# Later table loads, fewer early fill products and a DMA queue in program order in a two-block fp32 transformer kernel

## The chip, the cores and the metric

The kernel runs on one core of one Trainium2 chip. The metric is the device time of one execution in microseconds (us), lower is better. PE is TensorE, DVE VectorE, ACT ScalarE, POOL GpSimd, and SP is SyncE, whose queue issues all the kernel's transfers from HBM.

## The reference

Two blocks follow each other on one sequence of 256 tokens of 1024 features, all in fp32. The first has two layers of window attention and differential attention side by side, between an input product of 1024 x 4096 and an output product. The second has two layers (`DEPTH` is 2): sparse attention in the first, latent attention in the second, each with a cross-attention to a memory of 256 rows, and a block of 16 experts behind each.

```python
for l in range(DEPTH):                               # first block
    h = rmsnorm(x, norm_g[l])
    proj = h @ w_in[l]                               # 1024 x 4096
    ...
    x = x + y @ w_out[l]
x = rmsnorm(x, final_g)
for i in range(DEPTH):                               # second block
    proj = x @ nsa_w_in[j] if kind == 0 else x @ mla_w_in[j]
    ...
    mkv = mem @ mem_w_kv[i]
    xa = memory_cross_attention(xq, mk, mv).reshape(B, S, XA_WIDTH)
    y = jnp.concatenate([mix, xa], -1) @ w_out[i]
    x = layer_norm(DEEPNORM_ALPHA * x + y, ln_g[i, 0], ln_b[i, 0])
    f = hier_moe(x, ...)                             # 16 experts, 2 of them for each token
    x = layer_norm(DEEPNORM_ALPHA * x + f, ln_g[i, 1], ln_b[i, 1])
```

An expert is `silu(x @ w_gate) * (x @ w_up)`, times its gate, `@ w_down`: three matrices of 2 MB, so 96 MB for the 16 experts of a layer.

## The kernel before

**Products.** A projection (`Proj`, line 253 issues its products) splits both sides into a high and a low part that PE multiplies at its fast fp32 rate, and makes three products for each. `Emit.split` makes the weights' parts: ACT casts the high part (`wsp`, line 134), DVE subtracts for the low one (line 135). The parts of the activations are `xTh` (ACT, line 350) and `xTl` (DVE, line 352), made from `xraw`, the transposed input. A step of a `Proj` is one tile of 128 input features; `add_two` runs the first two projections together, four steps of one, four of the other, and so again.

**Order of work.** `Flow` holds a list of steps. `flow.before(s, fn)` calls a function ahead of step `s`, `flow.after` behind it; a step number below zero is a place ahead of the first product. PE, DVE and ACT run in the order in which the code calls them (`manual_schedule(engines=ENGINES)`). SP is not in that set: the framework's scheduler orders its queue. SP issues one transfer after another, and a transfer waits, with all behind it in the queue, until its tile is free and until the eighth transfer ahead of it has landed.

**Tables.** `constants2` loads positions and norm gains (`loads`, at step -10), and computes from the positions the angles of the rotations on DVE, one piece ahead of each of the steps 5 to 11.

**Experts.** The 192 loads of 512 KB of a layer's expert weights are handed out by the class `Weights`. There are three kinds of places: a ring of 12 tiles (`w`), and slots of 512 KB (`b4`) and of 1 MB (`b8`), shared with the activations (both show as `wa`). When a slot's weights have been read, `Weights.read` frees it and loads the next ones into it, as far as `others`, a table of what else will want the slots at which step, allows. When a ring tile has been read, the next load of the ring is called there. How many ring loads are under way is set ahead of the experts: `nsa_layer` calls twelve for the first layer, `mla_layer` three for the second. The tiles are handed out round the ring, so that with three under way the other nine are free.

**Between the layers.** Near the end of the first experts (step 237) `tail[0]` starts `memory_kv`, which loads the memory and its weights and makes `mkv` in small items of two products; `some(n)` in `mla_layer` takes n items at a time to fill PE. `tail[1]` loads the first part of the latent attention's input weights (`w_in`), in the last quarter of the last expert. At the block's end stands a branch (`tc.If`, line 2584) for experts with more than 64 tokens; here it isn't taken, and SP waits at it for the transfers under way.

## Time and profile before

| | us |
|---|---|
| median of 3 runs | 1007.44 (1005.86 to 1008.91) |
| the profiled execution | 1008.35 |
| its span in the trace | 1006.6 |
| PE busy | 978.5 |
| DVE busy | 644.2 |
| ACT busy | 433.4 |
| moved by DMA | 286.66 MB, 285 GB/s over the span |

The time of an execution has 1.75 us more than the span of its trace. PE's busy time and its gaps make up the span; what DVE, ACT and the DMA do counts where PE waits for it. The experts' products begin at 453 us in the first layer and at 783 in the second; the second layer's attention lies from 666 to there, and PE's last product ends at 995.7.

### The profile page before, as it was taken

To read this page: it belongs to the slowest core of one execution; us is meant where nothing else is said; L and a number is where in the kernel's file an instruction comes from. 1 tells how busy PE (TensorE), PEld (TensorE's weight loads), DVE (VectorE), ACT (ScalarE), POOL (GpSimd) and SP (SyncE) were. 2 spreads that over 40 slices of the span, in tenths; PEclk is the share of its full clock that TensorE was granted. 3 is DMA by queue.
4 is the path that set the end of the run, shared out by engine and by line. 5 is a ranking of instruction groups with operands and counts; after the bars stand their busy time and mean duration, and the time that the engine had idled before them with its cause. 6 is when DMAs were issued, how large, how long until landed. Compare 5 with 4: busy or idle time off the path is not lost. (4 is left out here: it accounts for less than half of the span.)

```text
span 1006.6 us, 16077 instructions
## 1 busy us (share of the span) xinstructions
PE 978.5 (97%) x5627; PEld 645.7 (64%) x5627; DVE 644.2 (64%) x1816; ACT 433.4 (43%) x1072; POOL 19.1 (2%) x38
## 2 busy tenths in 40 slices
PE   8999999999999989999999999999999999999994
PEld 7997889888898866784343443368878443434332
DVE  5766886567966788748465545458885656553545
ACT  6556665556664467634212121234883321212121
POOL 0000000000100000000000000000000000000000
PEclk9999999999999999999999999999999999999998
DMA  8964575543576584797999999986698799999995
GB/s 287 377 200 128 155 252 172 164 127 125 157 225 206 154 214 128 225 377 262 379 409 409 408 409 409 399 295 218 210 349 324 273 343 409 408 409 409 408 407 170
DMA packets 110873, 286.66 MB, mean 285 GB/s; under 512 B 14208, under 2 KB 30912, under 8 KB 110272
## 3 DMA queue, kind: packets, MB, share of 16 engines
q1 hardware_dynamic: 110784, 285.55, 79.3%
q8 instruction: 47, 0.77, 0.3%
q14 instruction: 42, 0.34, 0.1%
HBM read 284.46 MB, written 1.05 MB: 284 GB/s over the span
## 5 line engine op out<-in xcount | busy, mean ns | idle before, releaser
L2201 PE MATMUL eg<-wa,xg 128*64 128x512 f32 x796 | 210.6, 597 | 0.2 <-DMA wa<-moe_w_up_dram 0.2
L135 DVE TENSOR_TENSOR wsp<-w,wsp 128x512 fp32r<-128x512 f32 (+4 forms) x256 | 164.8, 658 | 64.0 <-ACT wsp L134 62.6
L253 PE MATMUL pj<-xTh,wsp 128*128 128x256 f32 x768 | 155.2, 292 | 3.5 <-DVE wsp L135 3.2
L134 ACT CAST wsp<-w 128x512 fp32r<-128x512 f32 (+4 forms) x256 | 142.7, 595 | 16.7 <-PE pj L253 7.6
L253 PEld LDWEIGHTS pj<-xTh,wsp 128*128 128x128 f32 x768 | 124.6, 193 | 10.3 <-issue 4.4
L2201 PEld LDWEIGHTS eg<-wa,xg 128*64 128x64 f32 x796 | 60.8, 136 | 102.2 <-issue 90.0
L253 PE MATMUL pj<-xTl,wsp 128*128 128x256 f32 x384 | 109.2, 284 | 0.0
L253 PE MATMUL pj<-wsp,xTh 128*128 128x512 f32 (+3 forms) x352 | 108.4, 389 | 0.0
L2211 DVE SCALAR_TENSOR_TENSOR z<-z,eg 64x512 f32<-64x512 f32 x32 | 21.7, 679 | 133.3 <-ACT z L2208 133.3
L2208 ACT ACTIVATE z<-eg 64x512 f32<-64x512 f32 x32 | 18.9, 592 | 174.5 <-PE eg L2201 174.5
L2241 PE MATMUL dn<-wa,hT 128*64 128x512 f32 x360 | 86.2, 593 | 0.2 <-DMA wa<-moe_w_down_dram 0.2
L2221 DVE SCALAR_TENSOR_TENSOR hq<-z,gall,eg 32x128 f32<-32x128 f32 x240 | 83.3, 347 | 4.1
L253 PE MATMUL pj<-wsp,yTh 128*128 128x512 f32 x240 | 77.7, 405 | 0.0
L2201 PE MATMUL eg<-w,xg 128*64 128x512 f32 x228 | 77.6, 597 | 0.0
L253 PEld LDWEIGHTS pj<-xTl,wsp 128*128 128x128 f32 x384 | 74.2, 193 | 0.4
L2251 ACT CAST ys<-dn 64x512 fp32r<-64x512 f32 x60 | 34.9, 581 | 85.3 <-PE dn L2241 79.8
L253 PEld LDWEIGHTS pj<-wsp,xTh 128*128 128x128 f32 x352 | 62.8, 188 | 11.6 <-issue 2.5
L253 PE MATMUL pj<-wsp,xTl 128*128 128x512 f32 (+3 forms) x176 | 66.7, 379 | 0.0
L2241 PEld LDWEIGHTS dn<-wa,hT 128*64 128x64 f32 x360 | 25.6, 137 | 52.1 <-issue 44.5
L405 ACT ACTIVATE z<-z,mx 128x256 f32<-128x256 f32 (+1 forms) x104 | 48.4, 470 | 15.9 <-DVE mx L396 15.9
L2256 DVE TENSOR_TENSOR ys<-dn,ys 64x512 fp32r<-64x512 f32 x60 | 41.3, 688 | 15.0 <-ACT ys L2251 13.9
L253 PEld LDWEIGHTS pj<-wsp,yTh 128*128 128x128 f32 x240 | 43.1, 188 | 9.1 <-issue 1.6
(424 smaller groups left out, 1440.5 us busy)
## 6 DMA issues: line engine op xcount, KB each, us to landing
wa<-moe_w_up_dram SPq DMA_DIRECT2D x101, 512.0 KB, 10.2
wa<-moe_w_gate_dram SPq DMA_DIRECT2D x98, 512.0 KB, 10.2
wa<-moe_w_down_dram SPq DMA_DIRECT2D x94, 512.0 KB, 10.2
w<-w_in_dram SPq DMA_DIRECT2D x64, 512.0 KB, 4.6
w<-moe_w_down_dram SPq DMA_DIRECT2D x34, 512.0 KB, 10.2
w<-moe_w_gate_dram SPq DMA_DIRECT2D x30, 512.0 KB, 10.2
w<-moe_w_up_dram SPq DMA_DIRECT2D x27, 512.0 KB, 10.1
w<-w_out_dram SPq DMA_DIRECT2D x24, 512.0 KB, 3.7
```

The costliest lines, as they stand in the source:

```text
L134: self.nc.scalar.copy(hi, src)
L135: self.nc.vector.tensor_sub(lo, src, hi)
L253: nc.tensor.matmul(o, a, b, start=begin and i == 0, stop=last and i == 2, skip_group_check=True)
L405: E.nc.scalar.activation(z[i], (src or z)[i], AF.Exp, bias=mx[:, i:i + 1], scale=1.0 if src else -1.0, accum_out=sm[:, i:i + 1])
L2201: self.E.nc.tensor.matmul(self.ps[b * CAP:b * CAP + CAP], self.xg[:, k, self.j], w, start=k == 0, stop=k == KD - 1, skip_group_check=True)
L2208: self.E.nc.scalar.activation(self.th, self.ps[:CAP], AF.Tanh, scale=0.5)
L2211: self.E.nc.vector.scalar_tensor_tensor(self.th, self.th, 1.0, self.ps[:CAP], op0=OP.add, op1=OP.mult)
L2221: self.E.nc.vector.scalar_tensor_tensor(self.hq[32 * q:32 * q + 32, :, h], th[:, q], self.gate()[r], u[:, q], op0=OP.mult, op1=OP.mult)
L2241: self.E.nc.tensor.matmul(self.pd[n * CAP:n * CAP + CAP], self.hT[:, k], self.w[2][k](0)[:, 512 * n:512 * n + 512], start=k == 0, stop=k == 3,
L2251: self.E.nc.scalar.copy(self.y[r, n], self.pd[r])
L2256: self.E.nc.vector.tensor_sub(self.y[o, n], self.pd[r], self.y[r, n])
```

## The change

Four edits. At the start: 8 warm-up products instead of 12, the first weights in two transfers of one feature tile each (`load_first`), `xraw` of the last four feature tiles ahead of the loads of `x`, its parts two and one steps earlier, squares and norm rows a little later, and the tables behind the second half of both first projections, with their angles five steps later. In the second layer's attention: two `mkv` items instead of three in seven opening steps, more in the last steps of the projection `pq`. At the end of the first experts: `tail[1]` is called with `tail[0]`, ahead of the branch, and nine `b4` slots are kept for it instead of five. And SP joins the engines that run in program order in the main part of both blocks of experts.

```diff
@@ -523,15 +523,15 @@
     norm.raw = raw = E.b8((KD, S), "xraw")
     load_xT(0, 2)
     nc.sync.dma_start(ng, a["norm_gT"])
-    E.warm(12)
+    E.warm(8)
     norm.begin()
-    norm.parts(0)
-
-    for s, fn, v in ((-15.7, load_xT, (2, 4)), (-15.5, load_x, (0,)), (-13, load_xT, (4, 8)), (-12.5, load_x, (1,))):
+
+    for s, fn, v in ((-15.8, load_xT, (2, 4)), (-13, load_xT, (4, 8)), (-12.5, load_x, (0,)), (-12.2, load_x, (1,))):
         flow.before(s, fn, *v)
+    flow.before(-3, norm.parts, 0)
     for i in range(4):
-        flow.before((3, 4, 6, 7)[i], norm.squares, i // 2, i % 2)
-    for k, s in ((2, 0), (4, 4), (6, 5)):
+        flow.before(5 + i, norm.squares, i // 2, i % 2)
+    for k, s in ((2, 0), (4, 2), (6, 4)):
         flow.before(s, norm.parts, k)
     fgT = const.tile([P, KD], F32, name="fgT")
     subg = const.tile([P, 2], F32, name="subg")
@@ -638,7 +638,15 @@
           for i, out, feature in ((0, qa_out, True), (1, k_out("ka"), True), (2, v_out("va"), False),
                                   (4, q_out("qb"), True), (5, k_out("kb"), True), (6, v_out("vb"), False),
                                   (3, ga_out, True), (7, gb_out, False))]
-    norm.rows(flow, s0 + 5 if l else s0 + 8, 5 if l else 4)
+    norm.rows(flow, s0 + 5 if l else s0 + 9, 5 if l else 3)
+    if l == 0:
+        def load_first(v, k0, nk):
+            for k in range(0, nk, 1 if k0 == 0 else nk):
+                n = 1 if k0 == 0 else nk
+                w = a["w_in"][0][(k0 + k) * P:(k0 + k + n) * P, :512]
+                nc.sync.dma_start(v[:, k:k + n], w.rearrange("(k p) c -> p k c", p=P))
+
+        ps[0].src = load_first
     Proj.add_two(flow, *ps[:2])
     for p in ps[2:]:
         p.add(flow)
@@ -836,12 +844,12 @@
     t = {}
 
     def loads():
-        nc.sync.dma_start(E.lnT, a["ln_T"])
-        nc.sync.dma_start(E.lnP, a["ln_P"])
         pos_i = const.tile([P, 3], I32, name="pos_i")
         nc.sync.dma_start(pos_i, a["pos"])
         t["pos"] = const.tile([P, 3], F32, name="pos"), pos_i
         t["inv"] = E.bcast(a["inv"], 24, "inv")
+        nc.sync.dma_start(E.lnT, a["ln_T"])
+        nc.sync.dma_start(E.lnP, a["ln_P"])
         t["rows"] = E.b4((S,), "rows")
         for h in range(2):
             nc.sync.dma_start(t["rows"][32 * h:32 * h + 32], a["ln_rows"])
@@ -911,9 +919,9 @@
     nc.scalar.activation(E.sin[:, 0, :16], E.mhalf, AF.Sin)
 
     it = angles()
-    for s in range(5, 12):
+    for s in range(10, 17):
         flow.before(s, next, it, None)
-    for s, fn in ((-10, loads), (13, sines), (15, rows)):
+    for s, fn in ((-7, loads), (17, sines), (19, rows)):
         flow.before(s, fn)
 
 
@@ -1639,7 +1647,7 @@
             E.free(ps)
 
     for _ in range(7):
-        step(lambda: some(3))
+        step(lambda: some(2))
     flow.before(0, rows)
     for i in (1, 0):
         flow.before(2, normalise, i)
@@ -1722,7 +1730,7 @@
     pq = Proj(E, [(0, win[:, 416:672])], 256, lambda: t["xT"], xq_out, True)
     flow.before(0, pq.load)
     for k in range(KD):
-        flow.steps.append((lambda k=k: pq.split(k), lambda k=k: (pq.mm(k), some(int(k < 10)))))
+        flow.steps.append((lambda k=k: pq.split(k), lambda k=k: (pq.mm(k), some(1 + (k > 3)))))
     pq.finish(flow, 23)
     flow.before(17, shared, 0)
     flow.before(18, shared, 1)
@@ -2116,7 +2124,7 @@
         self.others["b4"] += [(228, 2), (229, 1), (238, -2), (245, 1), (257, 2)]
         if i == 0:
             self.others["b8"].append((16 * NE - 19, 1))
-            self.others["b4"].append((16 * NE - 19, 5))
+            self.others["b4"].append((16 * NE - 19, 9))
         for v in self.others.values():
             v.sort(key=lambda e: (e[0], -e[1]))
 
@@ -2439,7 +2447,7 @@
 
             at(pre, s + 40, start)
 
-    with tc.manual_schedule(engines=ENGINES):
+    with tc.manual_schedule(engines=ENGINES | {mybir.EngineType.SP}):
         lg = columns()
         W.fill()
         E.warm(10)
@@ -2536,6 +2544,7 @@
                 work = tail[0]()
                 for g in work:
                     next(g)
+                tail[1]()
         assert not pre and not post, (pre, post)
 
 
@@ -2572,8 +2581,6 @@
             if q == 1:
                 parts(2, Y)
                 E.free(Y.y, *others)
-            if q == 1 and tail:
-                tail[1]()
             if q in (1, 2):
                 for t in range(2):
                     stats(q - 1, t)
```

**The start, ACT's queue.** Rows of before, then of the change, from the first parts of the input on (`wsp` are high parts of weights; `z` squares of `x`).

```order
L350 ACTIVATE xTh<-xraw,ng 128x256 x2
L134 CAST wsp<-w 128x512 x3
L350 ACTIVATE xTh<-xraw,ng 128x256 x2
L134 CAST wsp<-w 128x512 x3
L340 ACTIVATE z,ssq<-x 128x512
L134 CAST wsp<-w 128x512
L340 ACTIVATE z,ssq<-x 128x512
L350 ACTIVATE xTh<-xraw,ng 128x256 x2
L134 CAST wsp<-w 128x512
L350 ACTIVATE xTh<-xraw,ng 128x256 x2
```

```order
L350 ACTIVATE xTh<-xraw,ng 128x256 x2
L134 CAST wsp<-w 128x512 x3
L350 ACTIVATE xTh<-xraw,ng 128x256 x2
L134 CAST wsp<-w 128x512 x2
L350 ACTIVATE xTh<-xraw,ng 128x256 x2
L134 CAST wsp<-w 128x512 x2
L350 ACTIVATE xTh<-xraw,ng 128x256 x2
L134 CAST wsp<-w 128x512
L340 ACTIVATE z,ssq<-x 128x512
L134 CAST wsp<-w 128x512
```

The third pair of `xTh` moved from behind the seventh `wsp` to behind the fifth, and the squares from between the sixth and seventh to behind the eighth.

**The start, DVE's queue.** Rows of before, then of the change, from the fourth `wsp` on.

```order
L135 TENSOR_TENSOR wsp<-w,wsp 128x512 x4
L352 SCALAR_TENSOR_TENSOR xTl<-xraw,ng,xTh 128x256 x2
L135 TENSOR_TENSOR wsp<-w,wsp 128x512
L879 CAST pos<-pos_i 128x3
L881 TENSOR_SCALAR ang<-inv,pos 128x24 x3
L352 SCALAR_TENSOR_TENSOR xTl<-xraw,ng,xTh 128x256 x2
L135 TENSOR_TENSOR wsp<-w,wsp 128x512
```

```order
L135 TENSOR_TENSOR wsp<-w,wsp 128x512 x2
L352 SCALAR_TENSOR_TENSOR xTl<-xraw,ng,xTh 128x256 x2
L135 TENSOR_TENSOR wsp<-w,wsp 128x512 x2
L352 SCALAR_TENSOR_TENSOR xTl<-xraw,ng,xTh 128x256 x2
L135 TENSOR_TENSOR wsp<-w,wsp 128x512 x5
L368 TENSOR_TENSOR ssq<-ssq 128x2
L147 TENSOR_SCALAR rs_r<-ssq 128x2
L374 TENSOR_SCALAR rdiag<-ident,rs_r 128x128 x2
L135 TENSOR_TENSOR wsp<-w,wsp 128x512
L887 CAST pos<-pos_i 128x3
L889 TENSOR_SCALAR ang<-inv,pos 128x24 x3
L135 TENSOR_TENSOR wsp<-w,wsp 128x512
```

The cast of `pos` moved from behind the eighth `wsp` to behind the thirteenth.

**The second layer's attention, ACT's queue.** Rows of before, then of the change, at the last weights of the projection `pq` (`w` of 256) and the first of the next one (288).

```order
L1665 ACTIVATE z,mssq<-cs 128x128
L134 CAST wsp<-w 128x256 x3
L134 CAST wsp<-w 128x288
L1013 COPY mkv<-mkv 128x512
L134 CAST wsp<-w 128x288 x2
L1689 ACTIVATE cTh<-tp,cg 128x256 x3
L134 CAST wsp<-w 128x288
```

```order
L1673 ACTIVATE z,mssq<-cs 128x128
L134 CAST wsp<-w 128x256 x2
L1014 COPY mkv<-mkv 128x512
L134 CAST wsp<-w 128x256
L134 CAST wsp<-w 128x288 x3
L1697 ACTIVATE cTh<-tp,cg 128x256 x3
L134 CAST wsp<-w 128x288
```

The copy of `mkv` here is that of the second half in before and that of the first half now; the second half's moved behind these rows, past the scores on `xq`.

**The last experts, SP's queue.** Rows of before, then of the change, from the 13th load of the layer on (`w` goes to the ring, `wa` to slots).

```order
L2161 DMA wa<-moe_w_gate_dram 128x1024
L2161 DMA wa<-moe_w_up_dram 128x1024
L2161 DMA wa<-moe_w_gate_dram 128x1024
L2161 DMA wa<-moe_w_up_dram 128x1024
L119 DMA w<-moe_w_down_dram 128x1024 x2
L119 DMA wa<-moe_w_down_dram 128x1024 x2
L2161 DMA wa<-moe_w_up_dram 128x1024
L2161 DMA wa<-moe_w_gate_dram 128x1024
L2161 DMA w<-moe_w_gate_dram 128x1024
L2161 DMA wa<-moe_w_gate_dram 128x1024
L2161 DMA w<-moe_w_up_dram 128x1024
L2161 DMA w<-moe_w_gate_dram 128x1024 x2
```

```order
L2169 DMA wa<-moe_w_gate_dram 128x1024
L2169 DMA wa<-moe_w_up_dram 128x1024
L2169 DMA wa<-moe_w_gate_dram 128x1024
L2169 DMA wa<-moe_w_up_dram 128x1024
L119 DMA wa<-moe_w_down_dram 128x1024 x2
L2169 DMA wa<-moe_w_up_dram 128x1024
L2169 DMA wa<-moe_w_gate_dram 128x1024 x2
L2169 DMA wa<-moe_w_up_dram 128x1024
L119 DMA wa<-moe_w_down_dram 128x1024 x2
L2169 DMA wa<-moe_w_up_dram 128x1024
L119 DMA wa<-moe_w_down_dram 128x1024 x2
L2169 DMA wa<-moe_w_gate_dram 128x1024
```

The rows to `w` left this stretch; the `wa` rows stand as before. In the change the fourth load to the ring of this layer comes behind the 46th to slots; in before there are twelve ring loads ahead of that place.

## Rows read from the trace of the kernel before

**Rows 1.** The page: PE's busy time; GB/s in 40 slices of 25.2 us.
```profile
PE 978.5 (97%) x5627; PEld 645.7 (64%) x5627; DVE 644.2 (64%) x1816; ACT 433.4 (43%) x1072; POOL 19.1 (2%) x38
...
GB/s 287 377 200 128 155 252 172 164 127 125 157 225 206 154 214 128 225 377 262 379 409 409 408 409 409 399 295 218 210 349 324 273 343 409 408 409 409 408 407 170
```

**Rows 2.** PE's waits over the span: us in total, times, longest.
```profile
PE pj L253 <- DVE wsp L135: 3.2, 2, 3.0
```

**Rows 3.** Windows: length, busy us of PE, PEld, DVE, ACT, POOL, clock, DMA, GB/s.
```profile
666.00:700.00 34.00, 34.00 (x196) 30.27 (x195) 24.17 (x66) 15.00 (x40) 1.81 (x2) 1.00 0.75 264
700.00:740.00 40.00, 36.05 (x258) 29.89 (x257) 35.16 (x134) 33.16 (x107) 0.92 (x3) 1.00 0.74 238
...
826.00:840.00 14.00, 14.00 (x68) 4.60 (x64) 6.12 (x14) 2.35 (x4) 0.00 (x0) 1.00 1.02 409
...
960.00:980.00 20.00, 19.19 (x80) 7.12 (x75) 8.85 (x18) 4.00 (x7) 0.00 (x0) 1.00 1.03 409
```

**Rows 4.** Timeline of PE, start: start, us, engine, line, operation, [idle before, releaser].
```profile
6.58 0.39 PE L253 MATMUL pj<-xTh,wsp 128*128 128x256 f32 x1 [0.25 <-ACT wsp L134]
...
7.30 0.50 PE L253 MATMUL pj<-xTh,wsp 128*128 128x256 f32 x2 [0.22 <-DVE wsp L135]
...
22.24 0.60 PE L253 MATMUL pj<-xTh,wsp 128*128 128x256 f32 x2 [3.00 <-DVE wsp L135]
```

**Rows 5.** Windows of the start, columns as in rows 3.
```profile
1.50:5.00 3.50, 3.46 (x16) 3.46 (x17) 0.01 (x1) 1.38 (x4) 0.88 (x6) 1.00 0.76 210
5.00:6.00 1.00, 1.00 (x9) 1.00 (x9) 0.88 (x2) 0.45 (x2) 0.00 (x0) 1.00 0.97 340
...
23.50:25.00 1.50, 1.50 (x9) 1.50 (x9) 1.47 (x6) 0.08 (x1) 0.39 (x1) 0.50 1.06 396
```

**Rows 6.** Timeline of DVE, start.
```profile
16.08 0.69 DVE L135 TENSOR_TENSOR wsp<-w,wsp 128x512 fp32r<-128x512 f32 x1
20.00 0.17 DVE L879 CAST pos<-pos_i 128x3 f32<-128x3 int32 x1 [3.23 <-DMA pos_i<-pos_dram]
...
21.50 0.69 DVE L135 TENSOR_TENSOR wsp<-w,wsp 128x512 fp32r<-128x512 f32 x1
```

**Rows 7.** Timeline of ACT, start; a cast behind a wait starts as its weights land.
```profile
11.82 1.15 ACT L134 CAST wsp<-w 128x512 fp32r<-128x512 f32 x2 [1.40 <-DMA w<-w_in_dram]
...
14.64 0.90 ACT L350 ACTIVATE xTh<-xraw,ng 128x256 fp32r<-128x256 f32 x2
...
17.26 0.62 ACT L134 CAST wsp<-w 128x512 fp32r<-128x512 f32 x1 [0.40 <-DMA w<-w_in_dram]
```

**Rows 8.** Timelines of PE, ACT and DVE, the second layer's attention.
```profile
698.17 0.60 PE L998 MATMUL mkv<-wkv,memT 128*128 128x256 f32 x2
...
702.01 1.14 PE L497 MATMUL sc<-mkv,xq 64*128 64x256 f32 x8 [1.88 <-DVE xq L1697]
...
698.80 0.59 ACT L1013 COPY mkv<-mkv 128x512 f32<-128x512 f32 x1 [5.14 <-PE mkv L998]
...
701.27 0.69 DVE L1697 TENSOR_SCALAR xq<-pj 128x512 f32<-128x512 f32 x1
```

**Rows 9.** Timeline of SP's queue, loads of the last experts' weights.
```profile
716.07 0.33 SPq L2161 DMA_DIRECT2D w<-moe_w_up_dram  x1
...
735.49 4.29 SPq L119 DMA_DIRECT2D w<-moe_w_down_dram  x2
...
813.24 0.33 SPq L2161 DMA_DIRECT2D w<-moe_w_up_dram  x1
...
829.69 0.33 SPq L2161 DMA_DIRECT2D wa<-moe_w_gate_dram  x1
830.99 0.33 SPq L2161 DMA_DIRECT2D wa<-moe_w_up_dram  x1
```

**Rows 10.** Timeline of PE, the last experts.
```profile
791.33 7.09 PE L2201 MATMUL eg<-wa,xg 128*64 128x512 f32 x32
...
984.74 1.08 PE L2241 MATMUL dn<-wa,hT 128*64 128x512 f32 x4 [0.23 <-DMA wa<-moe_w_down_dram]
```

## The prediction

> **What bounds the kernel now.** I read the page first: TensorE (PE) is busy for 978.5 us [rows 1] of the span of 1006.6, so a change can win only by closing PE's gaps, 28.1 us in all, and can lose by opening new ones. PE's list of waits says where the largest is: 3.2 us for `pj` on VectorE's `wsp` [rows 2], at the start of the program. Third I read the DMA rate by slices: it touches a ceiling twice, in the two blocks of experts, and lies between 210 and 349 GB/s in the six slices (150 us) ahead of the second [rows 1]. The windows give the ceiling as 409 GB/s, in each of six windows from 826 to 980 us, with PE busy beside it [rows 3]. So PE is the bound nearly everywhere, and in the last block of experts PE and the weights' transfers are both at their limit.
>
> **The start.** In before PE works from 6.58 us, stops for 3.00 us until 22.24 [rows 4], and then runs at the granted clock 0.50 [rows 5], the lower of its two levels. The cause stands in VectorE's queue: the cast of `pos` waited 3.23 us for its table's transfer and began at 20.00; the `wsp` that PE needed stands behind it, at 21.50 [rows 6]. Its weights were there by 17.26 [rows 7]. The change moves the tables behind the second half of the first two projections, and `pos` five `wsp` further back in VectorE's order.
>
> How early can the ninth step (the one that waited) start now? A step of the first projections is 12 products; eight of them took from 7.30, where the first products are through, to 19.24 (22.24 less the 3.00) [rows 4], 1.49 us each. The first weights come as two transfers of 256 KB, and I give the first product 0.5 us for that, so that five steps end at 7.30 - 0.5 + 5 x 1.49 = 14.25. Now a new wait: ScalarE's order has the `xTh` of feature tiles 4 and 5 ahead of the sixth `wsp`, where they stood behind the seventh. Their `xraw` now follows the fourth of the weights' transfers; as much data lies ahead of it as lay ahead of the transfer behind that of 11.82. From 11.82 to 17.26 four of 512 KB landed (weights, `xraw`, `x`, weights) [rows 7], 1.36 us each, so it lands at 11.82 + 1.36 = 13.2. In before the low part that follows such an `xTh` (started at 14.64 [rows 7]) was done at 16.08 + 0.69 [rows 6], 2.13 us later; now that is 15.3, and PE, whose first products of the step need only the high part, idles about 0.9 us. Steps six to eight end at 15.1 + 3 x 1.49 = 19.6. The ninth follows at once, since its weights land near 17.2 as before.
>
> In before the ninth step started at 22.24 and the slow stretch, 3.4 us until about 25.9, cost half its length more: as if it had begun at 23.9 at the full clock. The gain is 23.9 - 19.6 = 4.3, less 0.1 for a later chain behind it: **-4.2 us**. Bounds: -5.2 if `xraw` is in time (the ninth step at 18.7), -2.2 if it is 2 us late. Will the new gap lower the clock? A gap of 1.88 us [rows 8] left it at 1.00 in the window from 700 to 740 [rows 3], so I say no. `pos` itself now lands behind two more transfers, at 20.0 + 2 x 1.36 = 22.7, but the `wsp` behind it in VectorE's queue is wanted at 19.6 + 5 x 1.49 = 27.0: nothing is lost.
>
> Four warm-up products fewer: the first ran at half rate, as 16 records in the 3.5 us up to 5.00 and 9 in the next 1.00 show [rows 5]. Eight end near 5.0, a gap of about 1 us follows, and the clock may rise later. If the first products ran at half rate for 3.4 us (as long as the slow stretch behind 22.24), that would take 1.7 us, of which 0.9 would fill the new gap. Cost 0 to 0.8, taken as 0.
>
> **The second layer's attention.** The `mkv` products that fill PE's time come two items to a step instead of three in seven opening steps; the items saved go to the last steps of `pq` and to the keys. Their number is the same, so PE's work is the same. In before ScalarE waited 5.14 us at the copy of `mkv`, until PE had made the last of them; what stands behind that copy came late, so that `xq` came at 701.27 and PE waited 1.88 us for it [rows 8]. Now the copy of the second half stands behind `xq`. What is late next is `xq` itself: 0.69 us after its last product, of which an item of two `mkv` products (0.60 with their overlap [rows 8]) covers some; 0.4 stays. Gain 1.5, less 0.2 for a copy of 0.59 that now stands ahead of `kT` in ScalarE's queue: **-1.3 us** (0 to -1.9). With fewer items in the opening PE could run dry there: at most 7 x 0.60 = 4.2 us. It was busy for 34.00 of 34.00 us from 666 to 700 [rows 3], and the weights of that stretch are now asked for earlier; I take 0.
>
> **The end of the first experts.** The loads of `w_in` move ahead of the branch, at which SyncE's queue (SP) waits for the transfers under way. PE has the `mkv` items meanwhile (the same 34.00): 0. The last ten weight loads go to other slots, and SP passes them at the pace of a full DMA in either kernel: 0. In this block SP's order is the same in before and after up to those ten, so there the new order of SP does nothing at all.
>
> **The last experts.** Here is the term that decides. In before the scheduler drew the loads into the ring (`w`) forward in SP's queue, since all twelve ring tiles are free early: the fourth went out at 716.07, the fifth at 735.49, the fifteenth at 813.24 [rows 9]. In program order a ring load is emitted only when one of three ring tiles in flight has been read, so that now the fourth stands behind 46 loads of `wa`, where the thirteenth stood. **Nine loads of 512 KB** that were out by 810 us are now still to come. The loads of `wa` can't move up in their place: each waits for a slot that PE has to free.
>
> From 826 on the DMA is at its ceiling, a load each 1.28 us (829.69 to 830.99 and the like [rows 9]; 0.524 MB at 409 GB/s). PE uses a load up in four products, 32 of which took 7.09 us [rows 10], so 0.89 us: it eats up the lead that the early loads gave. At 984.74 it waited 0.23 us for a weight [rows 10], so the lead was used up by then. Nine loads x 1.28 = 11.5 us more of transfers after 826, and PE waits for what it has no lead for: 11.5 at most, less about 1 for loads that had some lead left. **+10.5 us** (8.5 to 11.5), in many short waits late in the block. The gains ahead of it take nothing from this, since the slots come free by as much earlier.
>
> The Trainium skill, page "DMA: Bandwidth & Descriptors", section "Where 436 GB/s comes from", says that transfers from HBM are bound at about 358 GB/s for a core. The trace disagrees, with 409 over 150 us; by the page's figure the nine loads would be an estimated 13.2 us.
>
> **Sum.** -4.2 - 1.3 + 10.5 = +5.0 us. The profiled execution took 1008.35 us (span 1006.6 and 1.75 around it), which makes 1013.4; it lay 0.9 above the median of the runs, 1007.44, so for a median the prediction is **1012.4 us**. About 0.3% (3.0 us) is what a measurement here can tell from no change: slower, but by little more than that.
>
> **Rivals.** A, slower (the forecast): 1012.4, with its own range from 1009.5 to 1015.5 by the bounds above.
> B, faster: the nine loads don't reach the end, and only the gains stay, 1007.44 - 5.5 = 1001.9. For it: ahead of 826 there is room on the DMA for more than nine loads (273 to 349 GB/s in the four slices before [rows 1]), if the loads of `wa` find free slots. Against it: the room is there because SP waits for slots, and the wait at 984.74 says that the lead was gone. It decides from four loads on: with no more than four missing (5.1 us) the gains pay for them.
> C, half: some of the missing loads are made good, because slots come free earlier than the full DMA could use them; a loss of 3 to 7, so 1005 to 1009.5, about 1007.
> D, far slower: PE's waits for weights pull its clock down. The window from 960 to 980, with 0.8 us of idle in it, kept 1.00 [rows 3], and so did the gap of 1.88; only behind that of 3.00 came 0.50. One fall costs 1.7 us by that row; four more make 1019.
> [...]
>
> **How the numbers follow.** A 0.60, B 0.23, C 0.13, D 0.04. Slower by over 0.3% are D and A but for its edge: 0.63. Faster is B: 0.23. Within are C and that edge: 0.14. The range takes in A, C and the most of B: 1001.5 to 1015.5.
>
> **What would show it.** Right: PE's waits on DMA `wa` and `w` sum to about 10 us, all behind 860; the fourth ring load goes out near 800 instead of 716; 409 GB/s lasts to the block's end. At the start: the 3.00 gone, about 1 us of idle at the sixth step, no 0.50 behind it. In the attention: the 1.88 falls under 0.6. Wrong: no such waits in the last 100 us (then B), a clock of 0.50 among the last experts (D), or PE idle between 666 and 690, which would take the attention's gain.

## The result, and the profile after

The changed kernel takes **1012.75 us** (median of 5 runs, 1012.14 to 1013.42) where the kernel before takes 1007.44 (5 runs, 1005.86 to 1009.25): a ratio of 1.0064, 95% interval 1.0045 to 1.0084; the quotient of these two medians, 1.0053, lies inside it. It is slower by 0.5 to 0.6%, and 0.35 us above the predicted 1012.4.

Where the time went is read best by laying the two traces over each other: each PE instruction of before is paired with the same one of after, and the difference of their starts is the *shift* at that point. Its steps say what each stretch won or lost:

| stretch (time in before) | shift at its end | won or lost there | forecast |
|---|---|---|---|
| start, to 40 us | -2.0 | **-2.0** | -4.2 |
| first layers and experts, 40 to 600 | -2.1 | 0 | 0 |
| end of the first experts, 600 to 666 | -4.3 | **-2.2** | 0 |
| second layer's attention, 666 to 716 | -5.8 | **-1.5** | -1.3 |
| to the middle of the last experts, 716 to 890 | -5.8 | 0 | 0 |
| last experts, 890 to 970 | +4.9 | **+10.65** | +10.5 |
| end, to 995 | +4.1 | -0.8 | 0 |

The page of after, PE's busy time and the GB/s in 40 slices of 25.3 us, answers to [rows 1]:

```profile
PE 985.4 (97%) x5619; PEld 645.8 (64%) x5619; DVE 643.3 (64%) x1816; ACT 432.5 (43%) x1072; POOL 18.5 (2%) x38
...
GB/s 276 360 245 126 176 230 177 157 126 126 159 226 202 155 213 163 211 337 319 391 408 409 408 409 408 396 306 163 272 206 231 327 392 408 409 409 408 409 408 179
```

PE is busy 6.9 us longer than in before, with eight instructions fewer. Nothing was added for it to do. Where the loss sits, PE gets through fewer products in its busy time: from 900 to 940 us in after 174 in 38.85 us, in before 198 in 40.00. So the page counts as busy what is in part a wait for weights. The five slices from the 28th (682 to 809 us) have a mean of 240 against 275 in before: 35 GB/s less over 126 us is 4.4 MB, some eight loads of 0.524 MB that the DMA has not moved by then.

PE's waits over the whole span of after (us in total, times, longest), against [rows 2]: the 3.2 us at `wsp` is down to three waits of 1.1 in all, and the waits for the experts' weights sum to under 2.

```profile
PE eg L2209 <- DMA wa<-moe_w_up_dram: 1.0, 5, 0.2
...
PE pj L253 <- ACT wsp L134: 0.5, 1, 0.5
...
PE pj L253 <- ACT xTh L350: 0.4, 1, 0.4
PE eg L2209 <- DMA wa<-moe_w_gate_dram: 0.4, 2, 0.2
...
PE pj L253 <- DVE wsp L135: 0.2, 1, 0.2
```

This list alone would have refuted the forecast. PEld, PE's weight loads, shows what it hides. Groups of PEld instructions from 900 to 960 us: count, busy and mean time, then the idle time before them by what ended it. First before:

```profile
L2201 PEld LDWEIGHTS eg<-wa,xg 128*64 128x64 f32 x136 | 9.3, 136 | 17.1 <-issue 15.1 <-DMA wa<-moe_w_gate_dram 0.9 <-DMA wa<-moe_w_up_dram 0.4
L2241 PEld LDWEIGHTS dn<-wa,hT 128*64 128x64 f32 x64 | 4.6, 137 | 9.1 <-issue 7.4 <-DMA wa<-moe_w_down_dram 0.6 <-DMA wa<-moe_w_up_dram 0.6
```

and after:

```profile
L2209 PEld LDWEIGHTS eg<-wa,xg 128*64 128x64 f32 x110 | 8.4, 136 | 21.4 <-issue 9.8 <-DMA wa<-moe_w_up_dram 7.6 <-DMA wa<-moe_w_gate_dram 3.3
L2249 PEld LDWEIGHTS dn<-wa,hT 128*64 128x64 f32 x56 | 4.0, 136 | 8.0 <-issue 5.3 <-DMA wa<-moe_w_down_dram 2.7
```

Waits for a transfer were 2.5 us there (0.9, 0.4, 0.6, 0.6) and are now 13.6 (7.6, 3.3, 2.7): 11.1 more in 60 us, the size of the loss. (These are the weights in slots; those in the ring add 2.9. Not all that PEld waits is lost to PE, so the two need not agree to the tenth.)

The windows of after answer to [rows 3] (busy us of PE, PEld, DVE, ACT, POOL, clock, DMA, GB/s). PE is still full from 666 to 700, and the ceiling of 409 holds beside a clock of 1.00 to the end.

```profile
666.00:700.00 34.00, 34.00 (x207) 29.71 (x206) 26.61 (x72) 17.54 (x49) 1.61 (x3) 1.00 0.70 234
700.00:740.00 40.00, 37.95 (x259) 30.62 (x258) 33.84 (x140) 34.19 (x108) 0.31 (x1) 1.00 0.69 229
826.00:840.00 14.00, 14.00 (x68) 4.74 (x66) 7.75 (x17) 2.75 (x5) 0.00 (x0) 1.00 1.03 410
960.00:980.00 20.00, 19.19 (x82) 6.89 (x80) 12.54 (x27) 5.38 (x9) 0.00 (x0) 1.00 1.03 409
```

SP's queue in after, the loads into the ring, against [rows 9]. Three go out behind 704, the fourth at 799.60 instead of 716.07, and six are out by 836, where fifteen were by 813.24: nine fewer.

```profile
704.48 0.34 SPq L2169 DMA_DIRECT2D w<-moe_w_gate_dram  x1
706.32 0.34 SPq L2169 DMA_DIRECT2D w<-moe_w_up_dram  x1
707.52 0.33 SPq L2169 DMA_DIRECT2D w<-moe_w_gate_dram  x1
...
799.60 0.50 SPq L2169 DMA_DIRECT2D w<-moe_w_up_dram  x1
800.15 1.85 SPq L119 DMA_DIRECT2D w<-moe_w_down_dram  x2
...
836.65 0.33 SPq L2169 DMA_DIRECT2D w<-moe_w_gate_dram  x1
```

The attention, against [rows 8]: on PE the scores `sc` start without a wait, and ACT's second copy of `mkv` stands 10 us behind them.

```profile
694.95 1.14 PE L497 MATMUL sc<-mkv,xq 64*128 64x256 f32 x8
...
704.89 0.59 ACT L1021 COPY mkv<-mkv 128x512 f32<-128x512 f32 x1 [0.73 <-PE mkv L1006]
```

The start, windows against [rows 5] and ACT's queue against [rows 7]. The 3.00 is gone and no 0.50 shows, but from 6 to 10 us PE makes 8 and 12 products in 2 us each. And ACT's casts wait for transfer upon transfer; the `xraw` of the last four feature tiles comes at 15.21, two us after the 13.2 of the forecast.

In before, the window from 8 to 10 had 19:

```profile
8.00:10.00 2.00, 2.00 (x19) 2.00 (x18) 1.32 (x4) 1.62 (x4) 0.00 (x0) 1.00 1.04 357
```

In after, two windows, and behind them ACT:

```profile
6.00:8.00 2.00, 2.00 (x8) 1.77 (x9) 0.81 (x2) 0.62 (x1) 0.00 (x0) 1.00 0.93 247
8.00:10.00 2.00, 2.00 (x12) 2.00 (x11) 0.42 (x1) 0.21 (x1) 0.00 (x0) 1.00 0.99 273
```
```profile
9.79 0.63 ACT L134 CAST wsp<-w 128x512 fp32r<-128x512 f32 x1 [2.09 <-DMA w<-w_in_dram]
11.21 0.91 ACT L350 ACTIVATE xTh<-xraw,ng 128x256 fp32r<-128x256 f32 x2 [0.80 <-DMA xraw<-xT_dram]
...
15.21 0.91 ACT L350 ACTIVATE xTh<-xraw,ng 128x256 fp32r<-128x256 f32 x2 [2.02 <-DMA xraw<-xT_dram]
```

### The profile page after: what moved, and what is told of

The parts are those of the page before. It is cut to its first block, busy times and chain, and to the rows that moved or that the text cites. A ratio compares the mean times of both kernels' runs of the same rounds, so it can differ in the third digit from the quotient of the medians.

```text
span 1011.1 us, 16058 instructions
## 1 busy us (share of the span) xinstructions
PE 985.4 (97%) x5619; PEld 645.8 (64%) x5619; DVE 643.3 (64%) x1816; ACT 432.5 (43%) x1072; POOL 18.5 (2%) x38
## 5 line engine op out<-in xcount | busy, mean ns | idle before, releaser
L2209 PE MATMUL eg<-wa,xg 128*64 128x512 f32 x788 | 215.1, 598 | 1.7 <-DMA wa<-moe_w_up_dram 1.0
L134 ACT CAST wsp<-w 128x512 fp32r<-128x512 f32 (+4 forms) x256 | 142.4, 593 | 13.2 <-PE pj L253 5.9
L2209 PE MATMUL eg<-w,xg 128*64 128x512 f32 x236 | 80.3, 598 | 0.4 <-DMA w<-moe_w_gate_dram 0.2
L2249 PEld LDWEIGHTS dn<-wa,hT 128*64 128x64 f32 x352 | 25.3, 137 | 50.3 <-issue 42.8
```

The costliest lines, as they stand in the source:

```text
L134: self.nc.scalar.copy(hi, src)
L2209: self.E.nc.tensor.matmul(self.ps[b * CAP:b * CAP + CAP], self.xg[:, k, self.j], w, start=k == 0, stop=k == KD - 1, skip_group_check=True)
L2249: self.E.nc.tensor.matmul(self.pd[n * CAP:n * CAP + CAP], self.hT[:, k], self.w[2][k](0)[:, 512 * n:512 * n + 512], start=k == 0, stop=k == 3,
```

## The experiments

The theory: the loss is the nine loads into the ring, late because SP runs in program order, and the rest of the change gains. The rivals: SP's order alone isn't it, or the number of loads isn't; and for the start, the late clock, the order of ACT, or the transfers. All won-or-lost numbers are shifts against the one trace of before; times are medians. The median of the kernel before, from the same chip, is 1005.6 us for b_sp_manual, a_sp_free, a_ring12 and a_warm12, 1006.3 for b_tables, a_parts, b_fill and a_best, and 1005.5 for the other four. after_again, before_again and b_fill have one run each. The stretch from 40 to 600 us, left out here, is 0 in all but after_again, which loses 1.6 there.

| kernel | start | 600 to 666 | 666 to 716 | 890 to 970 | us | ratio (95%) |
|---|---|---|---|---|---|---|
| changed | -2.0 | -2.2 | -1.5 | +10.65 | 1012.75 | 1.0045 to 1.0084 |
| after_again | -3.5 | -1.4 | -1.5 | +11.1 | 1014.17 | |
| before_again | -1.0 | -2.1 | 0.0 | 0.0 | 1003.11 | |
| b_sp_manual | -1.4 | -0.2 | 0.0 | +10.3 | 1015.26 | 1.0079 to 1.0121 |
| a_sp_free | -3.3 | -2.3 | +0.4 | 0.0 | 1002.27 | 0.9958 to 0.9987 |
| a_ring12 | -1.9 | -0.1 | -1.5 | +1.0 | 1003.27 | 0.9960 to 0.9986 |
| a_ring6 | -3.6 | 0.0 | -1.5 | +7.3 | 1007.98 | 1.0014 to 1.0040 |
| b_tables | -4.8 | -0.8 | 0.0 | +0.2 | 1002.45 | 0.9945 to 0.9981 |
| a_warm12 | -1.7 | -2.3 | -1.5 | +10.9 | 1012.56 | 1.0043 to 1.0079 |
| a_parts | -3.7 | -1.6 | -1.5 | +10.6 | 1012.18 | 1.0043 to 1.0079 |
| a_warm_parts | -3.5 | -2.6 | -1.5 | +10.5 | 1011.10 | 1.0043 to 1.0088 |
| b_fill | -1.0 | -0.3 | -1.1 | +0.2 | 1004.47 | |
| a_best | -4.9 | -1.5 | -1.5 | +0.8 | 1000.70 | 0.9933 to 0.9969 |

### SP's order alone, and the change without it

```diff
 # b_sp_manual: the kernel before, and
-    with tc.manual_schedule(engines=ENGINES):
+    with tc.manual_schedule(engines=ENGINES | {mybir.EngineType.SP}):
 # a_sp_free: the changed kernel, and
-    with tc.manual_schedule(engines=ENGINES | {mybir.EngineType.SP}):
+    with tc.manual_schedule(engines=ENGINES):
```

> The kernel before with SP in program order in the blocks of experts and nothing else changed. Theory: the loss alone, +9 to +11 us: 1016 to 1019. Within the first experts nothing moves, because SP's order there is the same. Rival (the loss needs the earlier start of the attention): +0 to +3, 1007 to 1010.

> The changed kernel with SP left to the scheduler in the blocks of experts (that one edit undone, all others kept). Theory: ring loads of the last experts are drawn forward again (fourth load to the ring before 720 us), the loss of 10.6 us is gone and the time is 1001 to 1004. Rival (the loss comes from the other edits, for example from slots kept longer): 1011 to 1014.

One word in one line carries the whole loss: put into the kernel before it costs 10.3 us in the last experts, taken out of the changed kernel it gives all of the 10.65 back. The time of b_sp_manual, 1015.26, is 0.7 below what was expected. In b_sp_manual SP's queue shows the gap in the ring's loads:

```profile
713.13 0.53 SPq L2161 DMA_DIRECT2D w<-moe_w_gate_dram  x1
803.98 0.70 SPq L2161 DMA_DIRECT2D w<-moe_w_up_dram  x1
```

Without SP the loads of `wkv` and `w_in` stand behind the branch again, and the attention gains nothing although the fill products are in their new order. In the trace of a_sp_free PE and ACT now wait for them:

```profile
667.24 1.13 PE L1002 MATMUL mkv<-memT,wkv 128*128 128x256 f32 x4 [0.68 <-DMA wkv<-mem_w_kv_dram]
...
669.75 0.54 ACT L134 CAST wsp<-w_in 128x416 fp32r<-128x416 f32 x1 [4.63 <-DMA w_in<-mla_w_in_dram]
```

### How many loads: a ring of three, six and twelve

```diff
 # end of mla_layer, in the changed kernel: a_ring12 (a_ring6: 6)
-    for _ in range(3):
+    for _ in range(12):
         W.load()
```

> The changed kernel with one line altered: ahead of the last experts twelve ring loads are called instead of three. SP stays in program order. Theory (depth: in program order only three ring tiles are in flight, so nine loads of 512 KB come late): the twelve ring loads go out by about 770 us as in the kernel before, PE's shift against the kernel before stays near -6 us through the last experts instead of turning from -5.8 to +4.9, and the time falls by 9 to 11 us, to about 1002 (1001 to 1004). Rival (program order as such: SP stands at a load whose slot is taken, with free ones behind it): no gain, 1011 to 1014.

> The changed kernel with six loads into the ring asked for at the end of the second layer's mixer instead of three (the run with twelve lost 0.9 us in the last experts, the changed kernel with three 10.7). By SP's order six loads then stand later than in the kernel before, where nine did. Theory (each late load is one more transfer at the ceiling, about 1.1 to 1.28 us): the shift of TensorE's instructions rises by 6.5 to 7.4 us between 910 and 960, and the time is 1008.5 to 1009.5. Rival (the early loads are a lead with a threshold, so that half of them is nearly enough): under 3 us, 1005. Second rival (only the order at the block's start counts, not the number): still 9 to 11 us, 1012.

In SP's order nine loads stand late with three, six with six, none with twelve. The last experts lose 10.65, 7.3 and 1.0 (the time of a_ring6, 1007.98, is 0.5 below what was expected, the shift of 7.3 within it). That is 1.18 us for each late load by the first and 1.22 by the second, close to a load at the ceiling (1.28 by [rows 9]); a lead that is enough at half, or a loss by the order alone, would not give the middle value.

What the DMA has moved says the same without counting places in a queue. Here are the windows (columns as above) from 716 to 840 us in before, and in after, a_ring6 and a_ring12 the same stretch of PE's work, each moved by its kernel's shift; they follow in this order:

```profile
716.00:840.00 124.00, 122.92 (x692) 76.99 (x692) 79.57 (x249) 59.48 (x150) 0.70 (x1) 1.00 0.91 324
```
```profile
710.21:834.21 124.00, 122.94 (x693) 77.01 (x693) 79.55 (x249) 59.25 (x150) 0.70 (x1) 1.00 0.81 288
```
```profile
710.90:834.90 124.00, 122.93 (x693) 77.01 (x691) 79.58 (x249) 59.28 (x150) 0.70 (x1) 1.00 0.84 300
```
```profile
712.50:836.50 124.00, 122.94 (x692) 77.02 (x692) 79.57 (x249) 59.29 (x150) 0.70 (x1) 1.00 0.89 318
```

36, 24 and 6 GB/s less over 124 us are 4.5, 3.0 and 0.7 MB, or 8.5, 5.7 and 1.4 loads of 0.524 MB: 1.25, 1.28 and 0.7 us lost for each. The 1.0 that a_ring12 still loses fits that: it is a little behind too, and why is not shown. So SP in program order costs little in itself; it costs 10.65 because `mla_layer` left the drawing forward to the scheduler.

The Trainium skill, page "DMA: Bandwidth & Descriptors", section "Where 436 GB/s comes from", has HBM bind at about 358 GB/s, one core's half of what a stack gives, which would make a late load an estimated 1.46 us. The windows of these runs disagree, with 409 for a program that uses one core.

### The tables alone

```diff
 # b_tables: the kernel before, with the changed order inside loads(), and
-    for s in range(5, 12):
+    for s in range(10, 17):
-    for s, fn in ((-10, loads), (13, sines), (15, rows)):
+    for s, fn in ((-7, loads), (17, sines), (19, rows)):
```

> The kernel before with one part of the change alone: the tables' loads go out behind the eighth pair of the first weights' transfers, the position table ahead of the others, and the angles, sines and row sums five, four and four steps later. My theory: the wait of 3.0 us at 19.24 goes, the clock of 0.50 behind it too, and no new wait comes, since the order of the first weights and of the input's transposed tiles stays: TensorE's instructions at 40 to 600 us come 4 to 5 us earlier, and the time falls by 3 to 5 us (about 1003). Rival (the start is bound by the weights' own transfers anyway): the wait moves to another transfer and the shift is under 2 us, as in the changed kernel.

The tables' move alone wins 4.8 us at the start, more than all the start's edits together, and a_best below, with the same start, has 4.9. By its time, 1002.45 against 1006.3, it wins 3.9: the trace of before that the shifts are taken against had a slow stretch there that three other traces of the same start don't have, as is shown below. Its windows, columns as above, are full, with 36 and 34 products in 4 us:

```profile
16.00:20.00 4.00, 4.00 (x36) 4.00 (x35) 2.71 (x6) 3.55 (x10) 0.00 (x0) 1.00 1.05 373
20.00:24.00 4.00, 4.00 (x34) 3.95 (x33) 3.26 (x12) 2.37 (x6) 1.08 (x1) 1.00 0.65 177
```

### What eats the start's gain

```diff
 # a_warm12 and a_warm_parts: the changed kernel, and
-    E.warm(8)
+    E.warm(12)
 # a_parts and a_warm_parts: the changed kernel, and
-    for k, s in ((2, 0), (4, 2), (6, 4)):
+    for k, s in ((2, 0), (4, 4), (6, 5)):
```

> The changed kernel with twelve warm-up products instead of eight. In the changed kernel PE's first products ran at half rate until about 10.2 us, in the kernel before the rate doubled near 5.4 us. Theory (the four products taken away and the gap of 0.5 us behind them keep the clock low): records come at the full rate from 5.4 us, PE then waits for xTh of tiles 4 and 5 at about 15.9, and the start gains 1 to 2.2 us against the changed kernel: 1010.5 to 1011.8. Rival (the clock would have stayed low anyway, or the late transfers bind): within 0.4 us of it, 1012.4 to 1013.2.

> The changed kernel with the second and third high parts of the transposed input back behind the fifth and seventh weight splits in ScalarE's order (steps 4 and 5 in place of 2 and 4). Theory (the changed kernel's start lost 2 us against the forecast because these high parts, which wait for a late transfer, stand ahead of weight splits): TensorE's wait near 11 us goes, and the shift at 40 to 450 us is -3 to -4.5 instead of -2.0; the time falls by 1 to 2.5 us to 1010 to 1012. Rival (the weights' transfers themselves come too late): the wait moves to a weight split, the shift stays at -2, the time stays at 1012.7.

> The changed kernel with both repairs of the start together: twelve warm-up products as before, and the high parts of the transposed input behind the fifth and seventh weight splits. Theory (the start's gain was lost to two things, each enough alone: products at half rate for some us because the clock rises late, and a wait of ScalarE at a late transfer that stops TensorE): no wait above 0.6 us, 18 to 19 products in 2 us from 8 us on, and the shift at 40 to 450 us -4.3 to -5; the time 1010.5 to 1011.5. Rival (the split of the first weights and the new order of the transfers cost as well): shift -3 to -3.8 as with the order alone.

With twelve warm-up products PE is fast from 6 us on (14 products from 6 to 8, with a gap in it), but that brings it sooner to the second pair of `xTh` (feature tiles 2 and 3), whose `xraw` is late. In a_warm12, PE's timeline and a window:

```profile
11.22 0.38 PE L253 MATMUL pj<-xTh,wsp 128*128 128x256 f32 x1 [1.31 <-ACT xTh L350]
...
12.00:14.00 2.00, 2.00 (x11) 2.00 (x11) 1.38 (x3) 0.65 (x2) 0.00 (x0) 0.50 1.03 405
```

The wait is 1.31 instead of 0.40, and behind it the clock falls to 0.50 (1.2 GHz): nothing won. With eight, PE is as fast in two of five traces (13 products from 6 to 8 in after_again, 14 in a_ring12), so the edit doesn't slow every execution. With ACT's old order (a_parts) the wait near 11 is 0.54 and the start gains 1.7 more than in the changed kernel's first trace; but after_again has -3.5 with no edit at all, so that this isn't shown to be the edit's doing, and the times don't differ. Both together give -3.5, where -4.3 to -5 was expected: the rival's figure. Of 4.8 us about 1.3 are missing even then, and what is left is the two transfers for the first weights, the new order of the transfers, and the later norm rows, for which PE waits 0.31 us at 24.32 (0.36 in a_parts, nowhere else). The windows from 2 to 10 us, first b_tables, then a_warm_parts:

```profile
2.00:10.00 8.00, 7.78 (x49) 7.55 (x48) 3.38 (x7) 4.18 (x10) 0.38 (x2) 1.00 0.94 302
```
```profile
2.00:10.00 8.00, 7.57 (x48) 6.96 (x47) 2.98 (x6) 3.25 (x8) 0.37 (x2) 1.00 0.89 279
```

Less has been moved in the same time (279 against 302 GB/s; 256 in the first trace of the changed kernel). Over all traces it is 256 to 291 in the eight with the new first transfers and 289 to 307 in the six with the old, so these transfers are the suspect. Neither the split nor the order was tried alone, and which of the two it is stays open.

What decides the start shows in the traces that leave it as the change has it. The third pair of `xTh` waits for the `xraw` of the last four feature tiles, and PE for the weights' parts behind it. First PE in after, then ACT and PE in a_ring6:

```profile
17.41 0.50 PE L253 MATMUL pj<-xTh,wsp 128*128 128x256 f32 x2 [0.22 <-DVE wsp L135]
```
```profile
13.59 0.91 ACT L350 ACTIVATE xTh<-xraw,ng 128x256 fp32r<-128x256 f32 x2 [2.24 <-DMA xraw<-xT_dram]
...
15.79 0.51 PE L253 MATMUL pj<-xTh,wsp 128*128 128x256 f32 x2 [0.23 <-DVE wsp L135]
```

PE goes on 2.20 us behind that `xTh` in both (15.21 in after), and so it does in after_again (13.68 and 15.88) and a_sp_free (13.94 and 16.14). The shift at 40 us follows the landing to 0.02 us: -2.02 for 15.21, -3.27 for 13.94, -3.55 for 13.68 and -3.63 for 13.59. In the fifth trace, a_ring12, it lands at 14.50 and the shift is 0.85 us worse than the other four would give; there PE waits 1.67 us for the second pair, and a clock of 0.50 follows. How fast PE was before does not show in the result. In a_ring6 it is as slow as in after (9 and 11 products from 6 to 8 and 8 to 10 us, with 8 and 12 in after) and gains 3.6:

```profile
6.00:8.00 2.00, 2.00 (x9) 1.78 (x10) 0.99 (x2) 0.62 (x1) 0.00 (x0) 1.00 0.98 295
8.00:10.00 2.00, 2.00 (x11) 2.00 (x11) 1.19 (x4) 1.31 (x3) 0.00 (x0) 1.00 1.02 372
```

### The same kernels once more

> The kernel before once more, for the same spread. In two kernels with the same start the instructions at 40 us came 1.0 and 1.4 us earlier than in the profile of before, without the clock of 0.50. If the wait of 3.0 us at 19.24 lowers the clock only in part of the executions, this one shows a shift of 0 or of -1 to -1.5 at 40 us, and nothing over 0.4 in the first experts, the attention and the last experts.

> The changed kernel once more, for the spread of one profile against another of the same kernel: the shift at 40 us against the kernel before was -2.0, in the first experts -2.2, among the last experts +10.65, in the second layer's attention -1.5. If these are the change's own, they come back within 0.3 us; if the first experts' -2.2 hangs on where the stream of transfers happens to stand, it comes back between -0.1 and -2.5.

The attention (-1.5) and the last experts (+11.1, 0.45 more) come back; the rest has a spread. The -3.5 at the start of after_again is not kept: ahead of the first experts, with PE busy up to there, the clock is at 0.50 from 438.7 to 442 us, and the shift goes from -3.5 to -1.9.

```profile
438.70:442.00 3.30, 3.30 (x17) 3.30 (x17) 1.90 (x9) 2.01 (x3) 0.00 (x0) 0.50 1.03 415
```

The stretch from 600 to 666 gave -2.1 in a second trace of the *unchanged* kernel, and 0.0 to -2.6 in the twelve kernels and traces beside it, whichever edits they have; SP's order of the experts' loads is the same there in before and after up to the last ten. What varies is how long PEld waits for weights. PEld groups from 600 to 655 us, in before and in before_again:

```profile
L2201 PEld LDWEIGHTS eg<-wa,xg 128*64 128x64 f32 x88 | 6.9, 136 | 14.2 <-issue 11.6 <-DMA wa<-moe_w_up_dram 2.1 <-DMA wa<-moe_w_gate_dram 0.5
```
```profile
L2201 PEld LDWEIGHTS eg<-wa,xg 128*64 128x64 f32 x84 | 6.6, 136 | 11.6 <-issue 11.3 <-DMA wa<-moe_w_up_dram 0.3
```

The 2.6 us of waits in the one are 0.3 in the other, about the difference of the two traces.

The start of before came 1.0 us earlier the second time, although its wait was longer. PE's timeline and a window of before_again, against [rows 4] and [rows 5]:

```profile
22.76 0.50 PE L253 MATMUL pj<-xTh,wsp 128*128 128x256 f32 x2 [3.56 <-DVE wsp L135]
...
23.50:25.00 1.50, 1.50 (x15) 1.50 (x14) 1.43 (x8) 0.62 (x1) 0.00 (x0) 1.00 1.04 397
```

15 products in 1.5 us at 1.00 (2.4 GHz) where the first trace has 9 at 0.50: the slow stretch that the forecast wanted to win back is there in one of four traces with this start.

### The fill products alone

```diff
 # b_fill: the kernel before, and
-        step(lambda: some(3))
+        step(lambda: some(2))
...
-        flow.steps.append((lambda k=k: pq.split(k), lambda k=k: (pq.mm(k), some(int(k < 10)))))
+        flow.steps.append((lambda k=k: pq.split(k), lambda k=k: (pq.mm(k), some(1 + (k > 3)))))
```

> The kernel before with one part of the change alone: the fill items (products of mkv) come two to a step in place of three in the second layer's opening, and the saved ones go to the last steps of pq. Theory A (the fill order alone takes away the wait of 1.88 us at 700): the shift of TensorE's instructions falls by 1.3 to 1.5 us between 666 and 716. Theory B (the weights asked for ahead of the branch are needed for it as well, as the run with SP free of the manual order suggests, where a wait for their transfer came in its place): the stretch gains 0 to 0.5 us, with TensorE or ScalarE waiting for wkv or w_in near 667 to 671.

They win 1.1 of the 1.5 us by themselves, between the two theories and nearer to A, and no wait for `wkv` or `w_in` takes the place. In this kernel PE comes to the stretch only 1.2 us earlier than in before. In a_sp_free it comes 5.6 us earlier with the loads in the same place behind the branch, and waits for them. By these two traces the loads ahead of the branch are what keeps the gain when PE is early.

### The best of the parts

```diff
 # a_best: the kernel before (its start, its first weights, its warm-up), with
 #   the tables' move as in b_tables, the fill items as in b_fill,
 #   tail[1] ahead of the branch, nine b4 slots for it, SP in program order, and
-    for _ in range(3):
+    for _ in range(12):
         W.load()
```

> A candidate for the best version: the kernel before with the tables' move, the new fill items, SP in program order with the next layer's weights ahead of the branch, and a ring of twelve loads in program order, but the first weights, warm-up and norm as before. If the gains add: start -4 to -5, attention -1.5, last experts 0 to +0.9, so 1000 to 1002.5 where the kernel before is at 1005.6 to 1007.4. If the gain of the start is lost to contention: about 1004.

1000.70 us, 0.9951 of the kernel before (0.9933 to 0.9969), faster than either kernel: the start's 4.9 and the attention's 1.5 are kept, and the last experts cost 0.8. Its page has PE busy for 9 us less than the changed kernel:

```profile
PE 976.4 (98%) x5627; PEld 643.8 (65%) x5627; DVE 642.7 (64%) x1816; ACT 432.4 (43%) x1072; POOL 18.9 (2%) x38
```

b_tables, with the tables' move alone, has 1002.45, and the intervals of the two overlap, so that it isn't shown which of them is faster.

## Why the prediction was right, point by point

**The last experts: right**, mechanism and size. +10.5 was forecast, and six traces with three loads under way have 10.3 to 11.1. Nine late loads, the fourth at 800 instead of 716, 409 GB/s to the block's end: each is in the rows. That "the gains ahead of it take nothing from this" holds too: the loss is the same where PE arrives 1.7 us early (b_sp_manual) and where it arrives 7.5 early (a_warm_parts). Rivals B and C fell with the 10.65 itself, and with a_ring6, where six late loads still cost 7.3. Rival D fell by the windows, which keep a clock of 1.00 among those waits.

**What would show it: half wrong.** The waits were to appear in PE's list; of some 11 us it has under 2. The rest lies in PE's busy time and shows on PEld. The idle time of about 1 us at the sixth step was 0.22, since PE came late to it.

**The attention: right.** -1.3 was forecast, and all eight traces with the new fill and the early loads have -1.5. The wait of 1.88 is gone and 1.5 of it was won; the 0.4 that was to stay at `xq` and the 0.2 for a copy were 0.2 too much together.

**The end of the first experts: right, though the first trace spoke against it.** 0 was forecast, the trace had -2.2, and a second trace of the unchanged kernel has -2.1.

**The start: the chain right, the landing wrong.** -4.2 was forecast, -2.0 came (-1.9 to -3.6 in five traces of that start). The step that failed is "So it lands at 11.82 + 1.36 = 13.2": the `xraw` landed at 15.21, and at 13.6 to 14.5 in the other four, since the first transfers moved less than before's. What hangs on it came as forecast: PE goes on 2.20 us behind it (2.13 in the sum), and the bound of -2.2 for an `xraw` 2 us late is near what the first trace shows. Two readings failed besides. The slow clock behind 22.24, taken as the kernel's own, is in one trace of four, so that some 1.6 of the gain hung on the one trace it was read from. And a lower clock behind a new gap, which the forecast ruled out, came in a_ring12, behind 1.67 us at an earlier step, and cost 0.85. "Cost 0 to 0.8, taken as 0" for the four warm-up products was not what failed: a_ring6 and a_sp_free have PE as slow up to 10 us as in after and gain 3.6 and 3.3. The tables' move, which the forecast credited, is worth 4.8 by itself against the first trace of before, and 4.0 against the mean of the four with the old start.

**Why the total fits: in part by luck.** In the two traces that the forecast and the result were read from, the start's miss of 2.2 is made up by the 2.2 at the end of the first experts, which the change did not make, and 0.8 more by the program's end (1.3 in before_again, with no edit). By means over traces the start gained 2.0 (-2.9 in five traces of the changed start, -0.9 in four of the old one), not 4.2. So of the forecast's +5.0 the sum should have come to 10.6 - 2.0 - 1.5 = +7.1, where the medians differ by 5.3. The median of before was 1007.44 in these five runs and 1005.5 to 1006.3 in the later groups of 15 to 24 runs, from which the changed kernel's 1012.75 is 6.4 to 7.3 away. The hit on the total is better than the working at the start deserves.

## What to carry to other kernels

A queue put into program order loses whatever the scheduler had drawn forward; count the transfers that move behind the point at which the DMA reaches its ceiling; here each cost about one transfer's time there. Write the lookahead out (here one number, 3 to 12) before the order is fixed. A wait for weights can hide in PE's busy time: look at PEld, and take a second trace of the unchanged kernel before a shift of 2 us is given to an edit. A term that hangs on when one transfer lands needs the spread of that landing: here 13.6 to 15.2 us in five traces of one start.

## What was not expected of the hardware

A wait of 3.56 us at the start left the clock at 1.00 in before_again, one of 3.00 was followed by 0.50 in the first trace of before, and ones of 1.67 and 1.31 were followed by 0.50 in a_ring12 and a_warm12. The one of 1.88 in the attention left it at 1.00 in the first trace of before, and was followed by 0.50 in before_again; PE's timeline there, and a window:

```profile
698.95 1.13 PE L497 MATMUL sc<-mkv,xq 64*128 64x256 f32 x8 [1.88 <-DVE xq L1697]
...
700.50:703.50 3.00, 3.00 (x14) 3.00 (x14) 1.85 (x6) 2.07 (x7) 0.00 (x0) 0.50 0.56 167
```

So the length of a wait does not decide by itself here, and the same wait of the same kernel went both ways. The Trainium skill, page "TensorE: Matmul & The Clock Gate", section "HAM oscillation — how this bites in real kernels", tells of a kernel whose waits of some 3 to 5 us for a transfer each put the clock back. The wait of 3.56 here did not. The last experts don't test it: none of PE's waits for their weights in after is over 0.2 us, and the clock stays at 1.00 among them. The windows of after:

```profile
900.00:940.00 40.00, 38.85 (x174) 14.35 (x172) 15.68 (x38) 8.20 (x16) 0.00 (x0) 1.00 1.03 408
940.00:980.00 40.00, 38.25 (x151) 13.49 (x150) 20.40 (x43) 7.72 (x13) 0.00 (x0) 1.00 1.03 409
```

From 6 to 10 us in the first trace of the changed kernel PE makes about half the products of before's pace while the clock column says 1.00. The count of products in a window, not the column, showed that it was slow.
